# Where recurrent tiles, pairs of heads and w1's first factors stand in the second half of an input projection

## The chip, the cores and the metric

The kernel runs on one core of a Trainium2 chip. The metric is the device time of one execution in microseconds. The core has five engines with a queue each: TensorE (PE; its weight loads are shown as PEld), VectorE (DVE), ScalarE (ACT), GpSimd (POOL) and SyncE (SP, which here only starts DMA transfers). Each engine works through its own instructions in the order of the program, and a wait of one instruction holds up all that stand behind it on that engine.

## The reference, cut to what matters

One decoder block on 2048 tokens of width 1024, in float32. Eight attention heads and a gated linear recurrence share an input projection and an output projection; a squared-ReLU MLP follows.

```python
def hybrid_mixer(h, w_in, conv_w, conv_b, w_r, b_r, w_i, b_i, lam, w_out):
    z = h @ w_in
    q, k, v, xr, gr = jnp.split(z, [512, 1024, 1536, 2048], axis=-1)
    attn = dilated_attention(q, k, v)
    xr = causal_depthwise_conv(xr, conv_w, conv_b)
    rec = rg_lru(xr, w_r, b_r, w_i, b_i, lam) * jax.nn.gelu(gr)
    return jnp.concatenate([attn, rec], axis=-1) @ w_out

h = rms_norm(x, mix_norm_pre);  m = hybrid_mixer(h, ...);  x = x + rms_norm(m, mix_norm_post)
h = rms_norm(x, mlp_norm_pre);  x = x + rms_norm(squared_relu_mlp(h, w1, w2), mlp_norm_post)
```

## The kernel before, in words

A float32 product is made of three products on TensorE: each operand is split into a high part (a rounded copy, made by ACT) and a low part (the difference, made by DVE or POOL), and hi·hi, hi·lo and lo·hi are added up. `product` (L190 to L201) makes one tile z of 128 columns of the projection by 512 tokens: 8 steps over the width times 3, so 24 matmuls.

The sequence is handled in two halves of 1024 tokens, two blocks of 512 each. The steps of the input projection are named by strings. `q` with a half and a pair of heads (`qkv`, L203) makes the pair's six tiles: q, k and v, two blocks each. Each z is evacuated to zn by DVE (L225, L228), q and k are split into zh (ACT) and zl, and both are stored to DRAM by SP (L235, L236); v is transposed on PE (L240), split and stored. zh and zl have one buffer each. `r` with a half and a tile (`recurrent`, L288) does one of four recurrent tiles of 128 channels: per block a product for xr, its convolution (POOL L307, DVE L310 three times), two small matmuls for the gates (pr L313, pi L315), activations on ACT, a scan on DVE (L331), and a second product for the gate gr (L335), whose GELU runs mostly on POOL (L338 to L340) and whose result POOL stores. `a` with a pair is attention of the first half. For each step the raw columns of the weights (wraw, 256 KB at a time) are loaded by SP and split into wH (ACT) and wL. The engine of the low splits of weights and of zl is `pj.lo`: POOL at first, DVE once it is set so.

The program of this part is put in order by a scheduler, engine by engine, from the order in which the steps are written. The steps stand in three strings, `ORDER` (up to `a3`), `BETWEEN` and `LATER`. Behind `ORDER` the attention's memory is closed, and a pool `g2` opened in its place: the tiles of `early_factors` live there.

Two more things belong to this stretch. `load_wo(0)` loads w_out's first copy, eight transfers of 512 KB on SP (L781), and splits them (ACT woH, DVE woL); its memory is that which `lst.close()` frees. The output projection, whose first product is m0_0_0 (L846), needs it. `early_factors(j)` for j = 0 and 1 makes sums and differences of quarters of w1 for the MLP that comes later: four loads er of 256 KB (SP, L993), four sums (DVE, L1008 and L1013), seven splits into high and low (ACT and DVE), and fourteen stores sf (POOL, L1004) of 256 KB. `copies` are 40 transfers from DRAM to DRAM that lay out w_out and w2, issued by POOL (L1536) a few behind each step.

Behind this stretch the columns of the mix are loaded (m0_..L, SP L818), and the rest of the block (output projection, MLP, attention of the second half) follows by an order written out by hand.

Of the kernel before, what the change touches and what calls it, by code (L numbers as in the profile page):

```python
# [37 lines left out]
def f32(ap):  # L38
    return ap.bitcast(F32)
# [12 lines left out]
def split(nc, hi, lo, src, lo_eng=None):  # L52

    return (nc.scalar.copy(out=hi, in_=src),  # L54
            (lo_eng or nc.vector).tensor_tensor(out=lo, in0=src, in1=f32(hi), op=ALU.subtract))  # L55
# [708 lines left out]
def split_there(nc, hi, lo, lo_eng=None):  # L764

    split(nc, hi, lo, f32(lo), lo_eng)
# [44 lines left out]
def mix_columns(nc, sh, scr, hf, order, t):  # L811

    mx = {}
    for g0 in range(0, KT, 4):
        n = f"{hf}_{t}_{g0}"
        hi, lo = sh.pair(f"m{n}", (P, 4, P))
        k0 = order[g0]
        sh.mixed = nc.sync.dma_start(out=f32(lo), in_=scr["mix"][hf][k0:k0 + 4, :, t * P:(t + 1) * P].rearrange("k p t -> p k t"))  # L818
        split_there(nc, hi, lo, nc.vector if hf and t == 0 else nc.gpsimd)
        for i, k in enumerate(order[g0:g0 + 4]):  # L820
            mx[k] = (hi[:, i, :], lo[:, i, :])
    return mx
# [164 lines left out]
def early_factors(nc, sh, scr, w1, j):  # L987

    v, g = nc.vector, nc.gpsimd
    raw = [sh.s(f"er{j}_{i}", (P, KH, P)) for i in range(4)]  # L990
    a11, a12, a21, a22 = raw
    for i, t in enumerate(raw):
        nc.sync.dma_start(out=t, in_=w1[2 * j + i // 2][:, (i % 2) * KH:(i % 2 + 1) * KH])  # L993
    yield
    f = {}

    def made(m, src=None):
        if src is None:
            split_there(nc, *f[m])
        else:  # L1000
            f[m] = sh.pair(f"e{j}_{m}", (P, KH, P))
            split(nc, *f[m], src)
        for d, t in zip(scr["f"][j, m], f[m]):
            g.dma_start(out=d, in_=f32(t).rearrange("p k t -> p (k t)"))  # L1004

    def sub(m, x, y, op=ALU.subtract):
        f[m] = sh.pair(f"e{j}_{m}", (P, KH, P))
        v.tensor_tensor(out=f32(f[m][1]), in0=x, in1=y, op=op)  # L1008

    sub(5, a21, a22, ALU.add)  # L1010
    sub(7, a11, a21)
    sub(6, f32(f[5][1]), a11)
    v.tensor_tensor(out=a21, in0=a12, in1=f32(f[6][1]), op=ALU.subtract)  # L1013
    made(7)
    yield
    made(6)
    made(5)
    yield
    for m, t in ((1, a11), (2, a12), (4, a22), (3, a21)):
        made(m, t)  # L1020
        yield
# [405 lines left out]
NJ = FT // 2  # L1427
# [5 lines left out]
def trunk(tc, x, xT, g1, g2, g3, g4, w_in, conv_w, conv_b, w_r, b_r, w_i, b_i, lam, w_out, w1, w2,  # L1433
          ident_d, sel_d, mask_a, mask_b, out):
    nc = tc.nc
    out = out[0].rearrange("(b m c) d -> b c m d", m=P, c=NC)

    def sb(name, side):
        return tc.tile_pool(name=name, bufs=1, side=side, reuse_waits="tile")
# [5 lines left out]
    with (  # L1445
# [16 lines left out]
        def halves(shape, dt, n, nm):  # L1462
            return [[d.tile(shape, dt, name=f"s{nm}{hf}_{i}") for i in range(n)] for hf in range(2)]

        scr = {
            "q": halves([2, 2, HD, HT], F32R, NP, "q"),
            "k": halves([2, 2, HD, HT], F32R, NP, "k"),
            "v": halves([HT, 2 * P], F32R, NP, "v"),
            "co": halves([2, 2, HT], F32, NP, "co"),
            "mix": [d.tile([KT, P, HT], F32, name=f"smix{hf}") for hf in range(2)],  # L1470
            "x2": [d.tile([P, D], F32, name=f"sx2{i}") for i in range(S // P)],
            "a": [[d.tile([P, 7, TB], F32, name=f"sa{hf}_{j}") for j in range(NJ)] for hf in range(2)],
            "b": [d.tile([P, 4, TB], F32, name=f"sb{j}") for j in range(NJ)],
# [10 lines left out]
        def bank(tag, name):  # L1484
            if tag in RINGS:
                turn[tag] += 1
                tag = RINGS[tag][turn[tag] % 3 - 1]
            return banks.tile([P, TB], F32, tag=tag, bufs=BANKS[tag], name=name)
# [3 lines left out]
        def load_wo(hf, between=lambda: None):  # L1492
            return load_w_out(tc, wst.enter_context(sb(f"wo{hf}", "right")), scr["wout"], hf, order, cst, between)

        with contextlib.ExitStack() as st:
            p1a = st.enter_context(sb("p1a", "left"))
            p1 = st.enter_context(sb("p1", "left"))
            lst = contextlib.ExitStack()
            pl = lst.enter_context(sb("lru", "left"))
            pj = Project(tc, p1, p1a, pl, bank, cst, scr, x, xT, g1, w_in)  # L1500
            pj.recurrent_consts(conv_w, conv_b, w_r, b_r, w_i, b_i, lam)
            with sb("x0", "right") as px:
                w = {12: pj.load_start(12, px)}
                w[16] = pj.load_w(0, 16, nc.vector, px)
                w[13] = pj.load_w(0, 13, nc.vector, px)
                pj.load_norm(0, px)
                w[17] = pj.load_w(0, 17, nc.gpsimd, px)
                pj.spread_norm(0)
                pj.load_x(1, px)
                pj.load_norm(1, px)  # L1510
                pj.spread_norm(1)
                pj.recurrent(0, (0, 1), w, px)
                pj.load_norm(2, px)
                pj.load_norm(3, px)
            products = [(t[0], *map(int, t[1:])) for t in f"{ORDER} {BETWEEN} {LATER}".split() if t[0] in "qr"]

            copies = [(scr["wout"][k], w_out[k]) for k in order]
            for j in range(NJ):
                copies += [(scr["w2"][j][:, 0], w2[2 * j][:, 0:TB]),
                           (scr["w2"][j][:, 1:3], w2[2 * j + 1].rearrange("p (a d) -> p a d", a=2))]  # L1520

            def run(steps):
                for kind, *arg in [(t[0], *map(int, t[1:])) for t in steps.split()]:
                    if kind == "q":
                        pj.qkv(*arg)
                    elif kind == "r":
                        pj.recurrent(arg[0], (arg[1],))
                    elif kind == "a":
                        attend(*arg)
                    else:  # L1530
                        pj.load_x(*arg)
                        pj.spread_norm(*arg)
                    n = 8 if kind == "r" and arg[0] else 1 if len(copies) > 2 * NJ else 0
                    with tc.issue_after(cst["pool"].ins):
                        for dst, src in copies[:n]:
                            nc.gpsimd.dma_start(out=dst, in_=src)  # L1536
                    del copies[:n]
                    if kind in "qr":
                        products.pop(0)
                        if products:  # L1540
                            nxt, hf, i = products[0]
                            pj.load_ahead(hf, i if nxt == "q" else 12 + i)

            place = {"S": ("B", "B"), "pT": ("T", "T"), "o": ("O", "T")}
            with sb("at0", "right") as pa:
                attend = attention(tc, pa, lambda k, n: bank(place[k][0], n), cst, scr, 0, mask_a, mask_b, pa)
                run(ORDER)
            pg = per.enter_context(sb("g2", "right"))
            sh = Shared(pg, bank)
            run(BETWEEN)  # L1550
            lst.close()
            wo = load_wo(0)
            pj.lo = nc.vector
            early = [early_factors(nc, sh, scr, w1, j) for j in range(2)]
            for step in LATER.split():
                run(step)
                for _ in range(5):
                    if early and next(early[0], True):
                        early.pop(0)
            for rest in early:  # L1560
                for _ in rest:
                    pass
            ready = [mix_columns(nc, sh, scr, 0, order, t) for t in range(2)]
        sh.px = per.enter_context(sb("px", "left"))

# [49 lines left out]
        with per, tc.manual_schedule(engines={mybir.EngineType.PE}):  # L1615
            end = half(0, wo, ready)
            with sb("y0", "left") as pl, sb("z0", "left") as p:
                rest = mlp_out(tc, sh, p, cst, scr, 0, w2, g4, out, pl)
# [22 lines left out]
            with sb("y1", "left") as pl, sb("z1", "left") as p:  # L1641
                rest = mlp_out(tc, sh, p, cst, scr, 1, w2, g4, out, pl)
# [7 lines left out]
FIRST = 0  # L1650
SH = 2
ORDER = "q00 r02 q01 a0 r03 q02 a1 q03 x2 x3 a2 q10 a3"
BETWEEN = "r10 r11 r12 r13"
LATER = "q11 q12 q13"


def _by_residue(t):
# [51 lines left out]
```

## Time and profile before

| | us |
|---|---|
| median of three runs | 2258.18 |
| the runs | 2260.91, 2258.18, 2255.2 |
| the profiled execution, its own time | 2260.29 |
| its span | 2258.5 |
| first product of r10, of q11, of the output projection | 365.6, 520.2, 635.8 |

The mean granted clock of TensorE is 0.984. The page gives the busy time of each engine over the whole span; the stretch that the change touches is 366 to 636 us, some 12% of it, and is read by windows. There, r10 to r13 run up to 520 us, with attention's last pair beside them, and q11 to q13 behind. The program's names have the half, tile and block in them: z1_15_0 is the product of half 1, column tile 15 (12 to 15 are xr of r10 to r13, 16 to 19 their gates; 1, 5 and 9 are q, k and v of pair 1), block 0.

### The profile page before, as it was taken

What the parts mean: (1) busy time and instruction counts of PE and PEld (TensorE: products, weight loads), DVE (VectorE), ACT (ScalarE), POOL (GpSimd) and SP (SyncE); (2) the same over time, 40 slices, a digit from 0 to 9 for tenths busy, and PEclk for the clock granted to TensorE, in tenths of its full rate; (3) what the DMA queues carried; (4) which work ended last, traced back from release to release, by engine and by line L of the source; (5) the groups of instructions that cost most, each with busy time, mean ns of one, the idle gap of its engine ahead of it and who ended that gap; (6) DMA issues with size and microseconds to landing.
All of it is one profiled execution on the core that took longest, in us unless ns stands there. A gap on an engine that the chain in (4) does not pass through costs nothing.

```text
span 2258.5 us, 30786 instructions
## 1 busy us (share of the span) xinstructions
PE 2173.0 (96%) x10264; PEld 1778.9 (79%) x10264; DVE 1508.6 (67%) x2908; ACT 1232.9 (55%) x2489; POOL 449.6 (20%) x541
## 2 busy tenths in 40 slices
PE   8999999989899999998999999889999999999998
PEld 6678878767788788887878887778878888888887
DVE  6757475987648777774667676776766556646456
ACT  7647464654434555554766665754455555654442
POOL 5543415454223001011001111103200000000003
PEclk9999999999999999999999999999999999999999
DMA  8365674645974677869677787867553444776665
GB/s 289 95 189 179 183 233 151 188 143 184 330 227 171 232 264 274 309 257 303 193 208 215 215 242 195 230 211 235 175 192 137 168 140 163 262 238 194 196 192 182
DMA packets 223313, 473.51 MB, mean 210 GB/s; under 512 B 23105, under 2 KB 77793, under 8 KB 216881
## 3 DMA queue, kind: packets, MB, share of 16 engines
q1 hardware_dynamic: 194384, 336.87, 47.8%
q0 software_dynamic: 28768, 134.66, 17.1%
q8 instruction: 81, 1.33, 0.2%
q14 instruction: 80, 0.65, 0.1%
HBM read 337.09 MB, written 151.13 MB: 216 GB/s over the span
## 4 chain that ended last, share of the span: by engine, by line
PE 72%; DVE 8%; DMA 7%; issue 4%; ACT 4%; SPq 1%; POOL 0%; DVEq 0%; ACTq 0%; POOLq 0%
PE o L1210 8%; PE o L1211 8%; PE o L1212 7%; PE za L1061 5%; PE za L1062 5%; PE za L1060 5%; PE z L198 3%; PE z L199 3%; PE z L200 3%; PE m L846 3%; PE m L848 3%; PE m L847 3%; PE zc L1061 2%; PE zc L1062 2%; PE zc L1060 2%
## 5 line engine op out<-in xcount | busy, mean ns | idle before, releaser
L198 PE MATMUL z<-hH,wH 128*128 128x512 f32 x640 | 261.9, 409 | 17.5 <-ACT wH L54 7.0
L199 PE MATMUL z<-hL,wH 128*128 128x512 f32 x640 | 260.0, 406 | 0.6 <-DVE hL L173 0.6
L200 PE MATMUL z<-hH,wL 128*128 128x512 f32 x640 | 258.8, 405 | 0.5 <-DVE wL L55 0.5
L198 PEld LDWEIGHTS z<-hH,wH 128*128 128x128 f32 x640 | 122.4, 191 | 53.6 <-ACT wH L54 7.4
L200 PEld LDWEIGHTS z<-hH,wL 128*128 128x128 f32 x640 | 122.3, 191 | 30.3 <-issue 4.5
L199 PEld LDWEIGHTS z<-hL,wH 128*128 128x128 f32 x640 | 122.4, 191 | 30.2 <-issue 3.9
L420 ACT ACTIVATE smB<-smB,stB 128x128 f32<-128x128 f32 (+3 forms) x128 | 71.6, 560 | 82.0 <-DVE stB L414 81.8
L1065 ACT ACTIVATE sq<-sq 128x512 f32<-128x512 f32 x93 | 58.8, 632 | 89.6 <-DVE sq L1069 89.6
L55 POOL TENSOR_TENSOR wL<-wraw,wH 128x512 fp32r<-128x512 f32 x58 | 82.3, 1435 | 77.0 <-ACT wH L54 50.0
L55 DVE TENSOR_TENSOR tlB<-pT_B,thB 128x384 fp32r<-128x384 f32 x96 | 57.1, 598 | 53.0 <-ACT thB L54 48.9
L1125 POOL DMA_DIRECT2D sa<-sq x31 | 16.5, 532 | 363.1 <-ACT sq L1066 352.5
L54 ACT CAST wH<-wraw 128x512 fp32r<-128x512 f32 (+1 forms) x81 | 47.2, 611 | 61.6 <-DMA wraw<-in_dram 30.8
L420 ACT ACTIVATE sm<-sm,stA 128x256 f32<-128x256 f32 (+1 forms) x128 | 63.1, 495 | 29.4 <-DVE stA L414 29.2
L1066 ACT ACTIVATE sq<-sq 128x512 f32<-128x512 f32 x124 | 76.2, 629 | 1.9
L1244 POOL TENSOR_TENSOR y<-y,g4b 128x512 f32<-128x512 f32 x8 | 12.4, 1579 | 259.4 <-ACT junk_y L84 259.4
L414 DVE CUSTOM_DVE_ANT_0 smB<-SB,mask_b 128x128 f32<-128x128 f32 (+3 forms) x128 | 59.3, 483 | 6.3 <-PE pT_B L393 5.3
L629 PE MATMUL oB<-thB,vb 128*128 128x256 f32 x192 | 48.6, 282 | 11.3 <-ACT thB L54 10.4
L54 ACT CAST thB<-pT_B 128x384 fp32r<-128x384 f32 x96 | 48.5, 510 | 18.4 <-PE pT_B L393 10.1
L55 DVE TENSOR_TENSOR tlA<-pT,thA 128x512 fp32r<-128x512 f32 (+1 forms) x64 | 42.3, 669 | 22.0 <-ACT thA L54 21.7
L393 PE MATMUL pT_B<-ident,smB 128*128 128x128 f32 x320 | 52.2, 279 | 2.6 <-DVE tlB L55 1.8
L414 DVE CUSTOM_DVE_ANT_0 sm<-S,mask_a 128x256 f32<-128x256 f32 (+1 forms) x128 | 47.4, 409 | 9.1 <-PE pT L393 4.0
L1061 PE MATMUL za<-hLT,f_5H 128*128 128x512 f32 x128 | 50.1, 391 | 2.0 <-DVE hLT L55 2.0
(606 smaller groups left out, 7054.6 us busy)
## 6 DMA issues: line engine op xcount, KB each, us to landing
sa<-as POOLq DMA_DIRECT2D x31, 1024.0 KB, 6.1
w1r<-in_dram SPq DMA_DIRECT2D x56, 512.0 KB, 3.7
sa<-sq POOLq DMA_DIRECT2D x31, 768.0 KB, 4.0
wraw<-in_dram SPq DMA_DIRECT2D x79, 256.0 KB, 3.5
place<-in_dram SPq DMA_DIRECT2D x14, 1024.0 KB, 7.2
sb<-place POOLq DMA_DIRECT2D x14, 1024.0 KB, 5.3
kh<-sk SPq DMA_DIRECT2D x24, 512.0 KB, 5.0
kl<-sk SPq DMA_DIRECT2D x24, 512.0 KB, 6.8
```

The costliest lines, as they stand in the source:

```text
L55: (lo_eng or nc.vector).tensor_tensor(out=lo, in0=src, in1=f32(hi), op=ALU.subtract))
L198: pe.matmul(z, hi[:, k, :], hh, start=(k == 0), stop=False)
L199: pe.matmul(z, hi[:, k, :], hl, start=False, stop=False)
L200: pe.matmul(z, lo[:, k, :], hh, start=False, stop=(k == KT - 1))
L414: v.tensor_tensor_reduce(out=sm[:, c0:c0 + w], in0=sp[:, c0:c0 + w], in1=mask[:, mask.shape[-1] - w:], scale=1.0, scalar=3.0e38, op0=ALU.a ...
L420: s.activation(out=sm[:, c0:c0 + w], in_=sm[:, c0:c0 + w], func=AF.Exp, scale=-1.0, bias=st[:, 0, u, cols[j]:cols[j] + 1], accum_out=st[:, ...
L1060: pe.matmul(o, hi[:, k], bh[:, k], start=start and k == 0, stop=False, skip_group_check=True)
L1061: pe.matmul(o, hi[:, k], bl[:, k], start=False, stop=False, skip_group_check=True)
L1062: pe.matmul(o, lo[:, k], bh[:, k], start=False, stop=k == KH - 1, skip_group_check=True)
L1210: pe.matmul(o, ah[:, ts], bh, start=fresh and j == 0, stop=False, skip_group_check=True)
L1211: pe.matmul(o, ah[:, ts], bl, start=False, stop=False, skip_group_check=True)
L1212: pe.matmul(o, al[:, ts], bh, start=False, stop=j == NJ - 1, skip_group_check=True)
```

## The change

The steps behind attention stood as r10 r11 r12 r13 | q11 q12 q13, with `load_wo`, the change of `pj.lo` to DVE and the early factors at the bar; the factors' pieces were written one after each step behind the bar and the rest at the end. Now they stand as r10 q11 r11 q12 r12 r13 | q13; the factors for j = 0 are written whole behind q11, those for j = 1 behind q12, and at the bar stay `load_wo`, `lst.close()` and the change of `pj.lo`. So q11's and q12's low splits of weights and zl are POOL's. The copies are issued six behind each step from q10 on, before eight behind each r of half 1.

```diff
-                    n = 8 if kind == "r" and arg[0] else 1 if len(copies) > 2 * NJ else 0
+                    n = 1 if len(copies) > 2 * NJ else 6 if kind in "qr" and arg[0] else 0
...
-            run(BETWEEN)
+            early = [early_factors(nc, sh, scr, w1, j) for j in range(2)]
+            for step in BETWEEN.split():
+                run(step)
+                for _ in early.pop(0) if step in ("q11", "q12") else ():
+                    pass
             lst.close()
             wo = load_wo(0)
             pj.lo = nc.vector
-            early = [early_factors(nc, sh, scr, w1, j) for j in range(2)]
-            for step in LATER.split():
-                run(step)
-                for _ in range(5):
-                    if early and next(early[0], True):
-                        early.pop(0)
-            for rest in early:
-                for _ in rest:
-                    pass
+            run(LATER)
...
-BETWEEN = "r10 r11 r12 r13"
-LATER = "q11 q12 q13"
+BETWEEN = "r10 q11 r11 q12 r12 r13"
+LATER = "q13"
```

On SP, before, w_out's loads (woL0_k) stand between q11's last stores and w1's first quarters (er0):

```order
L235 DMA sk1_1_84<-zh1_5_1_5557 64x512
L236 DMA sk1_1_84<-zl1_5_1_5558 64x512
L110 DMA wraw1_6_0_5771<-in_6_dram 128x512
L110 DMA wraw1_6_1_5775<-in_6_dram 128x512
L781 DMA woL0_4_5374<-swo4_205 128x1024
L781 DMA woL0_5_5372<-swo5_206 128x1024
```

On SP, with the change, the same loads stand at the end, behind q13's stores and the mix's columns:

```order
L818 DMA m0_2_0L_6374<-smix0_103 128x4x128
L235 DMA sk1_3_86<-zh1_7_0_6114 64x512 x2
L818 DMA m0_2_4L_6379<-smix0_103 128x4x128
L236 DMA sk1_3_86<-zl1_7_0_6115 64x512 x2
L235 DMA sk1_3_86<-zh1_7_1_6149 64x512 x2
L236 DMA sk1_3_86<-zl1_7_1_6150 64x512 x2
L781 DMA woL0_4_5966<-swo4_205 128x1024
L781 DMA woL0_5_5964<-swo5_206 128x1024
```

w_out has moved behind the stores of k of pair 3 (sk1_3), and behind m0_2_4L, which waits until the last store of a factor (sf of j = 1) has landed.

On SP, with the change, w1's quarters come behind the gate's weights of r13 (19) and the first of q13 (3):

```order
L110 DMA wraw1_19_0_5753<-in_6_dram 128x512
L110 DMA wraw1_19_1_5757<-in_6_dram 128x512
L110 DMA wraw1_3_0_5939<-in_6_dram 128x512
L993 DMA er0_0_4995<-in_15_dram 128x512
L993 DMA er0_1_4996<-in_15_dram 128x512
```

Before, they stood behind the w_out loads, ahead of q12's last weights; their tiles lie in the memory that attention's last pair used.

On DVE, before, the end of the factors of j = 0 lies among q12's work:

```order
L55 TENSOR_TENSOR e0_4L_5942<-er0_3_5660,e0_4H_5941 128x512
L55 TENSOR_TENSOR wL1_3_5932<-wraw1_3_0_5933,wH1_3_5931 128x512
L55 TENSOR_TENSOR wL1_3_5932<-wraw1_3_1_5937,wH1_3_5931 128x512
L228 TENSOR_TENSOR zn1_10_0_5884<-z1_10_0_5859,bc2_3290 128x512
L55 TENSOR_TENSOR e0_3L_5948<-er0_2_5659,e0_3H_5947 128x512
L55 TENSOR_TENSOR zl1_6_0_5807<-zn1_6_0_5804,zh1_6_0_5806 128x512
```

On DVE, with the change, the end of the factors of j = 1 lies among r13's work, ahead of the first zn of q13:

```order
L331 SCALAR_TENSOR_TENSOR xc1_3_0_5790<-r1_3_0_5799,state_278,i1_3_0_5801 128x512
L55 TENSOR_TENSOR wL1_7_6078<-wraw1_7_0_6079,wH1_7_6077 128x512
L55 TENSOR_TENSOR e1_4L_5542<-er1_3_5502,e1_4H_5541 128x512
L310 SCALAR_TENSOR_TENSOR xc1_3_1_5878<-xr1_3_1_5874,cw_222,xc1_3_1_5878 128x512
L55 TENSOR_TENSOR wL1_7_6078<-wraw1_7_1_6083,wH1_7_6077 128x512
L225 SCALAR_TENSOR_TENSOR zn1_3_0_6032<-z1_3_0_6007,bc2_3290 128x512
L332 COPY state_278<-xc1_3_0_5790 128x1
L310 SCALAR_TENSOR_TENSOR xc1_3_1_5878<-xr1_3_1_5874,cw_222,xc1_3_1_5878 128x512
```

Both blocks of factors now stand between the first convolution of r13 and that zn. On PE the order is the same up to r10's first product, and as long up to m0_0_0 but for one transpose; z1_3_0, z1_3_1, z1_7_0 and z1_7_1 of q13 follow each other in one and the same bank, since the other bank of products holds z1_19_1 until its evacuation (gr1_3_1), which stands late on DVE.

## The prediction

> **What bounds the kernel now.** I read the page's first part, then the windows by stage, then the waits of TensorE (PE), then single instructions.
>
> ```profile
> PE 2173.0 (96%) x10264; PEld 1778.9 (79%) x10264; DVE 1508.6 (67%) x2908; ACT 1232.9 (55%) x2489; POOL 449.6 (20%) x541
> ```
>
> PE is busy 96% of the 2258.5 us span, so a gain can only come from its gaps. The change reorders what runs between the first product of r10 (365.6 us) and the first product of the output projection (635.8). The windows cut that stretch at the starts of r10, r11, r12, r13, q11, q12 and q13 (columns: window, its length, then busy time of PE, PE's weight loads, VectorE = DVE, ScalarE = ACT, GpSimd = POOL, granted PE clock, DMA share, GB/s):
>
> ```profile
> 366.00:400.00 34.00, 34.00 (x182) 28.36 (x181) 23.98 (x49) 19.30 (x42) 16.85 (x20) 1.00 0.41 128
> 400.00:440.00 40.00, 37.56 (x211) 30.10 (x210) 35.15 (x81) 26.71 (x63) 12.56 (x12) 1.00 0.55 151
> 440.00:475.00 35.00, 30.79 (x134) 22.30 (x133) 31.98 (x48) 18.76 (x36) 27.29 (x30) 1.00 0.58 189
> 475.00:520.00 45.00, 37.36 (x189) 29.27 (x188) 39.21 (x69) 28.10 (x55) 23.51 (x28) 0.92 0.40 122
> 520.00:558.00 38.00, 38.00 (x182) 30.25 (x181) 28.10 (x46) 16.65 (x27) 15.09 (x15) 1.00 0.65 203
> 558.00:594.00 36.00, 33.79 (x147) 26.74 (x147) 26.69 (x43) 18.45 (x33) 10.35 (x17) 1.00 0.93 320
> 594.00:636.00 42.00, 38.08 (x159) 30.55 (x158) 16.86 (x27) 11.33 (x20) 10.37 (x17) 0.92 0.93 303
> sum 270.00, PE 249.58 PEld 197.57 DVE 201.97 ACT 139.31 POOL 116.01; mean PE 35.65 PEld 28.22 DVE 28.85 ACT 19.90 POOL 16.57
> ```
>
> Lost to PE: 270.0 − 249.6 = 20.4 us idle, and the clock at 0.92 in two windows, 0.08 × (45 + 42) = 7.0 us: **27.4 us** in all. Of these 17.9 lie in r11 to r13 (2.4 + 4.2 + 7.6 + 3.6) and 9.5 in q12 and q13 (2.2 + 3.9 + 3.4). In r11 to r13 DVE is busy 35.15 of 40, 31.98 of 35, 39.21 of 45. The waits of PE from 360 to 640 (line <- releaser: total, times, longest):
>
> ```profile
> PE pr L313 <- DVE xc L310: 5.8, 1, 5.8
> PE z L198 <- DVE zn L228: 3.9, 1, 3.9
> PE z L198 <- DVE gr L335: 1.9, 2, 1.5
> PE z L198 <- DVE xr L304: 1.7, 4, 0.9
> PE z L198 <- ACT wH L54: 1.7, 1, 1.7
> ```
>
> PE waits for DVE: in the r steps because DVE is saturated there, in q13 (3.9) for another reason, which the DVE's own rows show:
>
> ```profile
> 591.38 0.68 DVE L55 TENSOR_TENSOR e_3L<-er,e_3H 128x512 fp32r<-128x512 f32 x1
> 602.68 0.69 DVE L55 TENSOR_TENSOR zl<-zn,zh 128x512 fp32r<-128x512 f32 x1 [10.62 <-DMA sq<-zl]
> 603.48 0.69 DVE L228 TENSOR_TENSOR zn<-z,bc 128x512 f32<-128x512 f32 x1
> ```
>
> DVE sat 10.6 us in its queue on a zl split, whose single buffer was still being stored; the zn behind it held PE's bank.
>
> **The change part by part.** *Alternation.* q11 and q12 each need less of DVE than of PE (28.1 of 38, 26.7 of 36 above, the latter with w_out's and w1's splits in it). With one between each two r steps, DVE catches up. What stays in r10 to q12 I work out from one recurrent block (DVE's groups from 440 to 540 us, POOL's from 366 to 520: line, operation, tiles, count | busy, mean ns | idle before):
>
> ```profile
> L310 DVE SCALAR_TENSOR_TENSOR xc<-xr,cw,xc 128x512 f32<-128x512 f32 x15 | 14.2, 947 | 0.1
> L331 DVE TENSOR_TENSOR_SCAN xc<-r,state,i 128x512 f32<-128x512 f32 x6 | 8.7, 1447 | 0.1
> L329 DVE SCALAR_TENSOR_TENSOR i<-i,xc 128x512 f32<-128x512 f32 x5 | 6.3, 1261 | 6.5 <-ACT i L320 6.5
> L343 DVE SCALAR_TENSOR_TENSOR ge<-ge,xc 128x512 f32<-128x512 f32 x5 | 6.2, 1234 | 0.0
> L327 DVE SCALAR_TENSOR_TENSOR th<-a,th 128x512 f32<-128x512 f32 x5 | 4.9, 971 | 0.1
> L326 DVE TENSOR_TENSOR a<-r 128x512 f32<-128x512 f32 x5 | 4.7, 931 | 0.7 <-ACT r L324 0.7
> L304 DVE TENSOR_TENSOR xr<-z,bc 128x512 f32<-128x512 f32 x4 | 4.3, 1077 | 0.0
> L330 DVE TENSOR_TENSOR i<-i,th 128x512 f32<-128x512 f32 x5 | 3.8, 766 | 0.0
> L55 POOL TENSOR_TENSOR wL<-wraw,wH 128x512 fp32r<-128x512 f32 x16 | 22.9, 1450 | 13.7 <-ACT wH L54 13.6
> L307 POOL TENSOR_SCALAR xc<-xr,cw,vec_cb 128x512 f32<-128x512 f32 x8 | 7.9, 988 | 6.0 <-DVE xr L304 5.9
> ```
>
> From a product's end to pr: 1.08 + 0.99 + 3 × 0.95 = 4.9 us. One product takes 5.6 us when nothing disturbs it (first and last of its 24 matmuls; the last two rows of this fence are the clock's after a gap and in q13's undisturbed end):
>
> ```profile
> 629.84 0.40 PE L198 MATMUL z<-hH,wH 128*128 128x512 f32 x1
> 635.21 0.39 PE L200 MATMUL z<-hH,wL 128*128 128x512 f32 x1
> 600.00:610.00 10.00, 6.08 (x18) 4.61 (x17) 7.13 (x12) 3.79 (x7) 1.59 (x3) 0.66 0.89 280
> 620.00:630.00 10.00, 10.00 (x44) 8.08 (x43) 1.20 (x3) 0.62 (x1) 0.00 (x0) 1.00 0.89 296
> ```
>
> So the chain hides behind the product that stands between, if DVE is on time. I leave about 1 us for each of the four blocks of r11 and r12, and 1 for a weight split like the 1.7 above: **5 us**. Below it is bounded by 2 (r10's window has no idle time at all), above by 9, half of what r11 to r13 lost.
>
> *zl and w splits to POOL.* q11's and q12's 8 zl and 12 wL splits leave DVE for POOL (20 × 1.45 = 29 us, in some 75 us). They hide behind products; and a zl that waits for its store no longer stands in DVE's queue. Without that cover each costs at most its 1.45 us once per weight, within the 9. The copies go out six a step from q10 on, before eight a step from r10 on, and stay hidden in POOL's idle time.
>
> The Trainium skill has a rule against this part: by its page "GPSIMD Engine Reference" (sections "1. Specifications" and "8. Key points"), GpSimd shares its SBUF interfaces with VectorE and contends with DVE instructions that have two SBUF inputs. The trace agrees as far as it goes: L310 takes 947 ns here, in windows where POOL computes, while the same size takes 0.68 us in e_3L's row above. By this rule DVE would be slowed 1.4 times under 29 us of POOL work, by some 8 us; without it by nothing.
>
> DVE has that time: 9.9 and 9.3 us idle in the two windows. The 9.5 us of q12 and q13, though, come back in other places, since w_out and w1's factors now meet r13 and q13.
>
> *w1's factors in r13.* The order on SP puts er0's loads behind the raw weights of r13 and q13, so they land some 8 us into r13. Let T be the start of r13's first product. The two blocks of factor work on DVE, eleven operations each, stand behind xc of 1_3_0 and around the scan of 1_3_0. One operation starts 0.60 us after the last (first two of the block in before):
>
> ```profile
> 580.96 0.69 DVE L1008 TENSOR_TENSOR e_5L<-er,er 128x512 f32<-128x512 f32 x1 [1.22 <-DMA er<-in_dram]
> 581.57 0.68 DVE L1008 TENSOR_TENSOR e_7L<-er,er 128x512 f32<-128x512 f32 x1
> ```
>
> Step by step: r13's first xc is done at T + 5.6 + 4.9 = 10.5. e0: 11 × 0.6 = 6.6, between them th, a, ge and i of 1_2_1 (0.97 + 0.93 + 0.7 + 1.26 = 3.9) and about 1.4 of waiting for ACT: 22.4. Then gr, xr, i, scan, ge (0.7 + 1.08 + 0.77 + 1.45 + 1.23 = 5.2): 27.6. Ten of e1's eleven operations (6.0), a, th, i, i, scan of 1_3_0 (0.93 + 0.97 + 1.26 + 0.77 + 1.45 = 5.4), two L310 (1.9), two wL and zn of q13 (2.0): zn1_3_0 ends at about T + 43. PE meanwhile has five products (28.0), four pr or pi (pi's eight records below are four blocks', 4.1 / 4 = 1.0, some of it beside other work; I take 0.9: 3.6), a wait of 2.4 for xc (which stands behind ACT's work for 1_2_1) and of 1.3 for gr: its z1_3_0 ends at T + 35.3.
>
> ```profile
> L315 PE MATMUL pi<-xc,bd_i 128*128 128x512 f32 x8 | 4.1, 598 | 0.0
> ```
>
> The next product must have the same bank, so it **waits 7.9 us**, where before it waited 3.9. After the 3.9 us gap the clock fell to 0.66 in the window of 600, 3.4 us; I take 2.9 here. Three more handings-on of that bank (before z1_7_0, z1_7_1 and z1_11_0) cost an operation of 0.68 each: 2.0. Sum: 2.4 + 1.3 + 7.9 + 2.9 + 2.0 = **16.5 us**.
>
> *w_out.* Before, its eight loads were issued behind q11's stores, their last split ended 57 us ahead of need:
>
> ```profile
> 559.51 10.16 SPq L781 DMA_DIRECT2D woL<-swo  x8
> 574.49 3.85 DVE L55 TENSOR_TENSOR woL<-woL,woH 128x512 fp32r<-128x512 f32 x6 [0.66 <-ACT woH L54]
> 570.00:580.00 10.00, 10.00 (x45) 8.08 (x44) 8.97 (x15) 6.05 (x11) 0.00 (x0) 1.00 0.98 351
> ```
>
> From 559.5 to 578.3 they took 18.8 us, at a DMA share of 0.98. Now they stand on SP behind the zl stores of 1_7_1, and behind m0_2_4L's load, which waits for the last factor store. 1_7_1's product ends at about T + 65; with zn, the zl split behind the one before it, and its store, the first w_out load is issued near T + 71. By 18.8 us the last split ends at T + 90; at 4 MB over 351 GB/s (11.9) and 3 for the splits, at T + 86. PE has 62.3 us of work from T on (ten products, 56.0; six pr or pi, 5.4; the transposes of v, 0.9) and comes to the output projection at T + 78.8 and needs the eighth factor 4.9 us later, at 83.7. Wait: 2.3 to 6.5, I take **4.5 us**.
>
> *Sum.* 27.4 removed; 5 + 16.5 + 4.5 = 26 put in their place: **1.4 us gained**, of the profiled execution's 2260.29 (span 2258.5). The median, 2258.18, is 2.1 lower; I subtract from it: 2256.8, say 2257. Bounds: at 0.68 an operation the recurrent ones are 4 us shorter up to zn1_3_0; with no loss of clock (2.9) and the short w_out wait, the tail is 21 − 4 − 2.9 − 2.2 = 12, and with 2 for the first part the gain is 13. At the other end the 21 factor operations run at 947 instead of 600 ns (7 us) and w_out waits 6.5: 30, with 9 in the first part 39, a loss of 12.
>
> **Rivals.** *The tail is short* (gain 13, **2245 us**): DVE has slack ahead of r13, so it starts there with nothing left over, and POOL mostly issues DMAs then, at which the e rows stay at 0.68. Against it: the fixed order and the single bank.
>
> *w_out decides* (slower, **2270 us**). Place: SP's queue ahead of the eight loads. From a first issue at T + 71 on, each us late is a us of PE's, and 6.8 us slower than before needs T + 79. What is late is the last factor store, on which m0_2_4L's load waits. Before it went out at 616.82 and took about 8 us, that is 55 us from er0's first load to its landing:
>
> ```profile
> 570.20 4.01 SPq L993 DMA_DIRECT2D er<-in_dram  x4
> 616.82 0.54 POOL L1004 DMA_DIRECT2D sf<-e_3L  x1 [0.42 <-DVE wL L55]
> sf<-e_3L POOLq DMA_DIRECT2D x2, 256.0 KB, 8.2
> ```
>
> With er0 at T + 2.4 this would be T + 57. It decides from T + 64, since the zl stores behind it take some 7 us more. If it lands at T + 77, 13 late, the time is 2256.8 + 13 = 2270. For it: the stores share the DMA with the wider traffic of q13; against it: 7 us of slack.
>
> *The alternation relieves nothing*: attention's third pair still runs beside r10 to r12, and POOL's 29 us slow DVE there. If r10 to q12 keep the 17.9 us of r11 to r13, time is 2256.8 + 12.9 = 2270. Against: PE's waits above name DVE, and q steps leave it idle. The rule of "GPSIMD Engine Reference" named above is this rival's, and the 0.95 against 0.68 us is all that the trace has for it.
>
> *It does not do what it says*: the factors are written behind q11 and q12, but stand behind r13's first xc on DVE. The time of that is already in the sum.
>
> **How the numbers follow.** Forecast 0.42; short tail 0.33; w_out 0.17; no relief 0.08. A measurement of this kernel tells about 0.3% from no change, 6.8 us. Faster by more: 0.34, all but a little of it the short tail; within: 0.41; slower: 0.25, the last two rivals. The range goes from 2241 to 2271: the bounds of the sum, a little further on the faster side for what the first part may give beyond 2; the forecast alone is 2250 to 2264.
>
> **What would show it.** Windows over r11 and r12 with PE over 95% busy: the alternation works; under 90%: no relief. The waits of PE in r13 and q13: z L198 <- DVE zn L225 of about 8 us once, pr <- xc of about 2.4. Under 3 us there, the tail is short. The first m L846 behind ACT or DVE wo L54/L55, or the DMA woL: 2 to 7 us as forecast, over 12 the slower rival. e operations starting 0.6 us apart: my price; 0.9: the upper bound. Above all wrong I would be if DVE came to r13 late, since every term there begins with its xr.

## The result and the profile after

The changed kernel takes 2270.47 us (median of 6, 2267.58 to 2281.33) where the kernel before takes 2256.69 (median of 6, the three runs shown above among them): a ratio of **1.0056, 95% interval 1.0038 to 1.0074**. It is slower by about 12.6 us by this ratio, 13.8 by the medians. The forecast was 2257, no change, in a range that reached to 2271: the time lies at the range's far end, and the forecast itself did not come.

The profiled execution has a span of 2265.8 us. The table of its windows is cut at the starts of r10, q11, r11, q12, r12, r13 and q13 (columns as before: window, length, busy time of PE, weight loads, DVE, ACT, POOL, granted clock, DMA share, GB/s):

```profile
363.00:390.00 27.00, 27.00 (x127) 21.69 (x125) 12.34 (x19) 9.45 (x13) 14.07 (x19) 1.00 0.54 187
390.00:448.00 58.00, 55.36 (x317) 46.15 (x316) 44.23 (x113) 37.25 (x98) 24.98 (x23) 0.97 0.66 200
448.00:478.00 30.00, 28.81 (x144) 23.21 (x143) 13.27 (x26) 12.01 (x26) 18.58 (x17) 1.00 0.44 141
478.00:527.00 49.00, 47.35 (x254) 38.11 (x253) 32.56 (x66) 26.66 (x59) 25.09 (x28) 1.00 0.63 191
527.00:551.00 24.00, 24.00 (x104) 18.97 (x104) 15.79 (x21) 7.18 (x12) 16.70 (x14) 1.00 0.44 138
551.00:589.00 38.00, 29.27 (x103) 20.81 (x102) 33.21 (x43) 18.46 (x27) 24.99 (x31) 0.87 0.69 235
589.00:642.00 53.00, 42.45 (x159) 31.91 (x158) 31.66 (x43) 22.59 (x35) 21.61 (x26) 0.90 0.74 230
```

Two things are to be seen. In the first five rows, r10 to r12, PE is idle for 5.5 us of 188 and its clock costs 1.7 more (0.03 × 58): the alternation keeps PE busy, 7.2 us lost. In the last two, r13 and q13, 8.7 + 10.6 us are idle and the clock costs 0.13 × 38 + 0.10 × 53 = 10.2: **29.5 us lost** in 91. The waits of PE from 360 to 700 us say on what:

```profile
PE z L198 <- DVE gr L335: 7.0, 3, 3.1
PE z L198 <- DVE state L332: 5.6, 1, 5.6
PE pr L313 <- ACT i L320: 4.8, 1, 4.8
PE m L847 <- DVE woL L55: 1.6, 7, 0.2
PE vt L240 <- DVE vs L55: 1.5, 1, 1.5
```

The wait of the gate's product (gr) comes three times, and the 5.6 us put down to `state` are a wait for zn1_3_0, which ends beside it (rows further below). The first output product is stretched by its waits for w_out's splits: it takes 9.3 us (642.16 to 651.43) where the next one takes 5.5, 3.8 more. So the loss is 7.2 + 29.5 + 3.8 = 40.5 us in place of 27.4, 13.1 more, about the change of the median. (Such sums count idle time inside a slow stretch of the clock twice: by the rows about 1.7 us here and 1.6 in the 27.4, so the difference stands. The two profiled executions differ by 7.3 us only: from r10's first product to the second output product this one takes 11.9 us longer, but it was 2.3 us ahead at r10's start already, and some 2 us came back behind.)

### The profile page after: what moved, and what is told of

Its sections match the earlier page's. It is cut to its first block, busy times and chain, and to the rows that moved or that the text cites. A ratio compares the mean times of both kernels' runs of the same rounds, so it can differ in the third digit from the quotient of the medians.

```text
span 2265.8 us, 30778 instructions
## 1 busy us (share of the span) xinstructions
PE 2173.3 (96%) x10264; PEld 1777.0 (78%) x10264; DVE 1492.4 (66%) x2888; ACT 1231.5 (54%) x2489; POOL 477.1 (21%) x561
## 4 chain that ended last, share of the span: by engine, by line
PE 60%; DVE 7%; DMA 6%; issue 4%; ACT 4%; POOL 1%; SPq 0%; DVEq 0%; ACTq 0%; POOLq 0%
PE o L1210 7%; PE o L1211 7%; PE o L1212 7%; PE za L1061 5%; PE za L1062 5%; PE za L1060 5%; PE zc L1061 2%; PE zc L1062 2%; PE zc L1060 2%; PE m L848 2%; PE m L847 2%; PE m L846 2%; PE oB L629 1%; PE z L198 1%; PE z L200 1%
## 5 line engine op out<-in xcount | busy, mean ns | idle before, releaser
L55 POOL TENSOR_TENSOR wL<-wraw,wH 128x512 fp32r<-128x512 f32 x70 | 99.7, 1441 | 89.9 <-ACT wH L54 61.2
L1125 POOL DMA_DIRECT2D sa<-sq x31 | 16.5, 533 | 362.4 <-ACT sq L1066 351.9
L414 DVE CUSTOM_DVE_ANT_0 smB<-SB,mask_b 128x128 f32<-128x128 f32 (+3 forms) x128 | 59.4, 483 | 10.6 <-PE pT_B L393 9.1
L629 PE MATMUL oB<-thB,vb 128*128 128x256 f32 x192 | 49.5, 287 | 12.9 <-ACT thB L54 11.9
L629 PEld LDWEIGHTS oB<-thB,vb 128*128 128x128 f32 x192 | 38.2, 199 | 18.8 <-ACT thB L54 14.9
```

What stands on the lines that cost most here:

```text
L629: pe.matmul(dst.rearrange("p (i m) -> p i m", m=P), vb[:, x * NC + c, :], t[:, cols].rearrange("p (i m) -> p i m", m=P)[:, ::step], start= ...
```

## The experiments

Three theories were put to the chip. **F**: w1's factors, set among r13's operations on DVE and ACT, hold PE. **W**: w_out's late loads hold it. **G**: GpSimd's tensor work slows DVE. All ratios are against the kernel before, run beside each experiment.

### Without the factors, their stores kept (e1, e2)

```diff
-    raw = [sh.s(f"er{j}_{i}", (P, KH, P)) for i in range(4)]
...
+    e = sh.s(f"er{j}_0", (P, KH, P))
+    nc.vector.memset(e, 0.0)
+    yield
+    for m in (7, 6, 5, 1, 2, 4, 3):
+        for d in scr["f"][j, m]:
+            nc.gpsimd.dma_start(out=d, in_=e.rearrange("p k t -> p (k t)"))
```

> The changed order, but w1's first factors are not made: no quarter of w1 is loaded, DVE does none of their 22 operations and ACT none of their 14 casts; the 28 stores stay and write a constant, so the MLP's result is not the reference's. Theory F (the factors' work on DVE and ACT stands between r13's own operations, and holds PE's pr, gr and zn): the waits and slow clock between r13's first product and the output projection fall from about 33 us to 8 to 12, the time from 2270 to 2245 to 2250. Rival W (w_out's late loads hold the end): 3 us at most, 2265 or more. Rival G (GpSimd's own tensor work slows DVE in r13): r13 keeps its waits, 2262 or more.

> The order before, with the same left out. Theory F: the factors stood under cover there, so the time falls by 0 to 4 us, to 2253 to 2257 (the wait of 3.9 us in q13 came from the store of zl). If the factors cost as much in both orders, it falls by as much as e1 does, some 20 us, and theory F is wrong in its place.

Measured: e1 1.0061 (1.0037 to 1.0085), e2 1.0045 (1.0022 to 1.0068). Theory F's numbers failed in both. The time of e1 lies where W and G had put it, but not for their reasons: the profile shows that the experiment brought a new cause. The waits of PE in e1 from 540 to 760 us, and a stretch of SP's queue:

```profile
PE pr L313 <- DVE xc L310: 26.8, 2, 24.0
...
591.20 20.70 SPq L110 DMA_DIRECT2D wraw<-in_dram  x4
```

Nothing paces the 28 stores any longer: POOL issues them in one train, from 564.6 to 585.7 us, ahead of r13's L307 in its own queue, and the next raw weights take 20.7 us to be issued. The runs say nothing on F. They show that the factors' arithmetic also spreads 7 MB of stores (28 of 256 KB) over time.

### Without the factors, their places filled early (e5, e6)

```diff
+            given = [(d, w1[m][:, 0:KH].rearrange("p k t -> p (k t)")) for j in range(2)
+                     for m in (7, 6, 5, 1, 2, 4, 3) for d in scr["f"][j, m]]
-                        for dst, src in copies[:n]:
+                        for dst, src in copies[:n] + given[:3]:
-            early = [early_factors(nc, sh, scr, w1, j) for j in range(2)]
...
```

> The changed order, w1's factors not made at all in this stretch: their 28 places in DRAM are filled early, three copies from w1 behind each of the steps up to a3, so the MLP's result is not the reference's. Theory F (the factors' work on DVE and ACT in r13 holds PE): the tail's waits and slow clock fall from 33 us to 8 to 12, the time is 8 to 13 us below the kernel before. Rival C (r13's own chain of xr, xc, gates and scan with one bank of products is enough to hold PE): 20 us or more stay, the time is that of the kernel before or up to 10 us above it.

> The order before, with the factors left out in the same way (early copies, no work). Theory F: they were under cover there, 0 to 5 us below the kernel before. If it falls by as much as e5 against the changed kernel, the place of the factors is not what cost.

Measured: e5 1.0044 (1.0027 to 1.0061), e6 1.0056 (1.0033 to 1.0079). Against both expectations the times went up, because the early copies cost in the steps up to a3: r10's first product starts at 377.1 us in e5 and at 381.0 in e6, where it started at 363.3 and 365.7. The stretch under study can still be read by itself, from r10's first product to the first of the output projection, in one profiled execution each:

| | with the factors | without | factors cost |
|---|---|---|---|
| order before | 365.65 to 635.79: 270.1 | 380.96 to 646.43 (e6): 265.5 | 4.6 |
| changed order | 363.33 to 642.16: 278.8, and 3.8 in the next product | 377.11 to 639.75 (e5): 262.6, and 0.8 in the next product | 19 |

Two readings. The factors cost 4.6 us under the cover they had, and 19 where the change puts them: some 14 us more, and the change cost 12.6. So F is right in size. And without the factors the changed order is only 2 us shorter than the order before, though the sum had 27.4 us of loss removed against 5 left in r10 to r12. Both are differences of single executions; two executions of one and the same kernel further below (e9 and e13) differ by 1.4 us in this stretch. The windows of e5 over r13 and q13, with its waits from 360 to 760, show what is left:

```profile
563.00:600.00 37.00, 28.24 (x104) 20.96 (x105) 26.20 (x29) 16.65 (x24) 19.87 (x20) 0.86 0.21 68
600.00:640.00 40.00, 38.07 (x156) 29.30 (x155) 28.73 (x40) 21.11 (x32) 8.06 (x8) 0.96 0.51 160
...
PE pr L313 <- DVE xc L310: 8.8, 1, 8.8
```

Counted as above the two steps lose 17.5 us, neither the 8 to 12 of F nor the 20 or more of rival C. Half of it is one wait of 8.8 us in r13. On DVE (first fence) and POOL (second) there stands:

```profile
563.26 7.71 DVE L310 SCALAR_TENSOR_TENSOR xc<-xr,cw,xc 128x512 f32<-128x512 f32 x2 [0.71 <-POOL xc L307]
```

```profile
564.29 1.28 POOL L55 TENSOR_TENSOR m_4L<-m_4L,m_4H 128x512 fp32r<-128x512 f32 x1
565.52 2.48 POOL L55 TENSOR_TENSOR wL<-wraw,wH 128x512 fp32r<-128x512 f32 x2
567.96 1.25 POOL L55 TENSOR_TENSOR m_0L<-m_0L,m_0H 128x512 fp32r<-128x512 f32 x1
569.17 1.25 POOL L55 TENSOR_TENSOR m_4L<-m_4L,m_4H 128x512 fp32r<-128x512 f32 x1
```

Two operations of 0.7 us take 7.7, until shortly after POOL's train of five ends at 570.4. Three of the five are splits of the mix's columns (m), which POOL does in the changed kernel only from 613.8 us on: without the factors their loads come at 551 us instead of 607. So this wait is in part a product of the experiment, and it is not shown that r13 would lose as much in the changed kernel. It opened theory G anew, in another form.

### The low parts on DVE (e3)

```diff
+            pj.lo = nc.vector
             early = [early_factors(nc, sh, scr, w1, j) for j in range(2)]
             for step in BETWEEN.split():
```

> The changed kernel with the low splits of weights and zl on DVE from r10 on instead of from q13 on, so that GpSimd does no splits in that stretch. Theory F: the factor work in r13 stays, and DVE gets more work in r10 to r13: 2268 to 2282. Rival G: DVE is no longer slowed by GpSimd, 2255 to 2262.

Measured: 1.0086 (1.0066 to 1.0106), 2280.77 us: in F's range. Giving the splits of weights and zl to DVE makes it slower; GpSimd keeps the gate's work and the splits of the mix's columns. From 360 to 660 us PE waits 15.7 us at one place:

```profile
PE z L198 <- DVE gr L335: 21.2, 2, 15.7
```

DVE isn't full there: in r13 (555 to 593 us of e3) it is busy 25.5 of 38 us. What holds gr is the order of its queue: a weight split, now DVE's, waits until 564.9 for its raw weights, and nine operations of the factors stand between it and gr at 575.9. So the run shows another cost of giving DVE the splits. It doesn't settle G.

### Fewer pairs between, two behind (e4), and r10 earlier (e8)

```diff
-BETWEEN = "r10 r11 r12 r13"
-LATER = "q11 q12 q13"
+BETWEEN = "r10 q11 r11 r12 r13"
+LATER = "q12 q13"
```

> The order r10 q11 r11 r12 r13, then w_out, w1's factors and q12 q13, written as before (copies and engine of the low parts too). Theory F: r11 to r13 keep about two thirds of their loss (12 of 17.9), the factors lie behind r13 with two pairs as cover: 2248 to 2257. Rival W: w_out's loads stand late on SP, behind q13's first store, and hold the output projection by 5 to 10 us: 2260 to 2266.

Measured: 1.0064 (1.0046 to 1.0081), 2275.24 us: a miss for F's number and for W's. Its waits from 540 to 760 us:

```profile
PE pr L313 <- DVE state L332: 8.2, 1, 8.2
PE z L198 <- ACT e_6H L54: 3.0, 1, 3.0
PE z L198 <- DVE zn L228: 2.3, 1, 2.3
PE m L846 <- ACT m_0H L54: 2.2, 1, 2.2
```

The three r steps in a row lose no less than before: pr waits 8.2 us here and 6.2 once more ahead of this window (to 522.7), where its longest wait in the kernel before was 5.8. The two pairs behind them, with the factors and w_out beside them, lose in three more places.

```diff
-ORDER = "q00 r02 q01 a0 r03 q02 a1 q03 x2 x3 a2 q10 a3"
-BETWEEN = "r10 r11 r12 r13"
+ORDER = "q00 r02 q01 a0 r03 q02 a1 q03 x2 x3 a2 r10 q10 a3"
+BETWEEN = "r11 r12 r13"
```

> The kernel before with r10 ahead of q10 and a3, beside attention's third pair instead of behind it. If DVE's saturation in r10 to r13 is what costs, one r step less there gives back 3 to 8 us. If attention beside r10 loses as much, no change or up to 5 us slower.

Measured: 1.0070 (1.0044 to 1.0096), 14 us slower, worse than either side gave. Of its waits from 360 to 660 us the largest are 7.2 (vt behind a split of v), 4.2 (pr behind the scan's state), 3.7 (zn) and 3.5 (pi behind ACT), spread over the stretch. No single cause was isolated.

### Factors held back behind r13 (e11, e12)

```diff
     for i, t in enumerate(raw):
+        v.tensor_copy(out=t[:, 0, 0:1], in_=gate[:, 0:1])
         nc.sync.dma_start(out=t, in_=w1[2 * j + i // 2][:, (i % 2) * KH:(i % 2 + 1) * KH])
...
```

> The changed order, but w1's factors are held back by their data: each tile of a quarter first gets one column copied from the last gate gr of r13, so that their loads, DVE's 22 operations and ACT's 14 casts stand behind r13 and among q13's work; w_out's loads come behind them, the mix's columns behind w_out. Theory F: r13 runs as in the experiment without factors, and q13's DVE has room: 6 to 15 us below the changed kernel, so within 5 us of the kernel before. If w_out and the factors' DMA hold the output projection then: m L846 or L847 waits over 8 us, and the time is that of the changed kernel.

> Both: factors held behind r13, gate on ACT and DVE. F and G2 together: 3 to 8 us below e11, 2 to 8 us below the kernel before.

Measured: e11 1.0131 (1.0100 to 1.0163), 2290.13 us, and e12 1.0129 (1.0091 to 1.0166), 2290.42. In e11 r13 runs better, as F had it, but the time is 20 us above the changed kernel: the wait of L847 that the expectation named came, and is longer. e12 is no faster than e11, so its expectation failed. Windows of e11 over r13, q13, and the stretch behind (626 to 664), the wait behind them, and SP's w_out loads:

```profile
555.00:582.00 27.00, 25.42 (x103) 18.88 (x102) 21.75 (x26) 12.45 (x17) 15.50 (x15) 1.00 0.35 108
582.00:626.00 44.00, 39.47 (x154) 30.13 (x152) 32.87 (x53) 20.24 (x30) 17.14 (x24) 0.92 0.59 197
626.00:664.00 38.00, 3.07 (x8) 1.89 (x9) 19.56 (x31) 16.04 (x29) 9.58 (x16) 0.56 0.98 343
...
PE m L847 <- ACT m_0H L54: 26.4, 1, 26.4
...
629.75 6.57 SPq L782 DMA_DIRECT2D woL<-swo  x8
```

Up to the end of q13's last product at 625.5, r13 and q13 now lose 1.6 + 4.5 us and 0.08 × 44 of clock, 9.6 instead of 29.5: most of that loss came with the factors' place in r13. But then PE stands still for some 35 us, while the DMA is at 0.98. Of these, 8.9 are a wait of q13's last transposes, whose v split stands on DVE among the second block of factors; 26.4 are the wait for the mix's columns. The second block's stores and w_out are moved there (w_out's last split begins at 653.1), and the mix's columns stand on SP behind them and behind the last store of v, so that their load is issued at 656.4 only: that end of the wait is the experiment's own order. In the kernel before, w_out and the factors began at 559.5 and had 76 us at a share of 0.93 until the output projection. So the reason that seems to lie below F is cover. The factors are 2 MB of loads and 7 MB of stores, and w_out, whose memory r13 has to free, is 4 MB; by the stretch before they fit under some 70 us of other work (an estimate), and the changed order has one pair behind r13, 42 us before, to give. That no place in the changed order would serve is not shown: two were tried. Put in r13, the factors hold PE by DVE and ACT; put behind it, they hold it by the DMA and the queues.

### zl on GpSimd (e7)

```diff
-                    self.cst["pool"] = split(nc, zh, zl, zn, lo_eng=self.lo)[1]
+                    self.cst["pool"] = split(nc, zh, zl, zn, lo_eng=nc.gpsimd)[1]
```

> The kernel before with one thing changed: the low part zl of q11 to q13 is made by GpSimd, not DVE, so a zl that waits for its buffer's store stands in GpSimd's queue. If the 3.9 us wait of q13 and the slow clock behind it (3.4) come from DVE's queue, 4 to 8 us below the kernel before. Rival: the wait goes to another place (GpSimd's factor stores, DVE beside a busy GpSimd): no change, within 3 us.

Measured: 1.0033 (1.0019 to 1.0048), 6 us slower, where one side gave 4 to 8 below and the other no change. The rival's mechanism is what is seen: PE's wait grew from 3.9 us to 6.7 (waits from 360 to 760; then POOL's queue, then DVE's):

```profile
PE z L198 <- DVE zn L228: 6.7, 1, 6.7
...
631.22 1.26 POOL L55 TENSOR_TENSOR m_0L<-m_0L,m_0H 128x512 fp32r<-128x512 f32 x1 [10.74 <-ACT m_0H L54]
...
633.73 0.69 DVE L228 TENSOR_TENSOR zn<-z,bc 128x512 f32<-128x512 f32 x1 [13.52 <-POOL zl L55]
```

In POOL's queue the zl of q13 stands behind a split of the mix's columns, which waits 10.7 us for its high part; DVE's next zn waits for that zl, and PE's bank for the zn. So the expected gain was eaten by another wait of the same kind. It is 2.8 us of the 6; of the rest, the same profile shows 2.5 at a transpose of v, and pr in r10 to r13, which this edit does not touch, waits 8.4 where it waited 5.8.

### The gate's work off GpSimd (e9, e13, e10, e14)

```diff
-        g.tensor_tensor(out=ge, in0=gr, in1=gr, op=ALU.mult)
-        g.tensor_scalar(out=ge, in0=ge, scalar1=0.044715, scalar2=1.0, op0=ALU.mult, op1=ALU.add)
-        g.tensor_tensor(out=ge, in0=ge, in1=gr, op=ALU.mult)
+        s.activation(out=ge, in_=gr, func=AF.Square, scale=0.044715 ** 0.5)
+        v.scalar_tensor_tensor(out=ge, in0=ge, scalar=1.0, in1=gr, op0=ALU.add, op1=ALU.mult)
```

> The kernel before, with GpSimd's three operations on the gate (square, scale and add, product: L338 to L340, about 2.9 us a block) replaced by a Square on ACT and one operation on DVE; the result is the same in another rounding. Theory G2 (a DVE operation that meets GpSimd's tensor work waits until that work ends; in the profile before, operations that overlap it are stretched by 31.9 us in all between r10 and the output projection, those that don't by 0.6): with some 23 us of GpSimd's work out of r10 to r13 the stretch falls to 20 or less, and the time by 3 to 8 us below the kernel before. Rival: DVE's count of operations is what fills r10 to r13: no change, or slower, by the 0.6 us a block that DVE gets in addition.

> The kernel of e9 again, with more rounds, beside e14. G2 (GpSimd's tensor work stretches DVE's operations in r10 to r13): 2 to 8 us below the kernel before, with an interval clear of 1. If e9's difference was chance: within 2 us.

> The changed kernel with the same gate on ACT and DVE. G2: 3 to 8 us below the changed kernel, 3 to 9 us above the kernel before. Theory F says the factors still stand in r13 and q13: not below the kernel before.

> The kernel of e9 with the first term of the convolution (L307, 0.8 us a block on GpSimd) on ACT too, so that GpSimd is left with the weights' and zl's low parts. G2: DVE's stretch falls again, by some 3 us; the time is 0 to 4 us below e13. Rival: ACT's queue (weight casts, tanh, table loads) makes xc later, and pr waits for it: 0 to 6 us above e13.

On the kernel before: e9 0.9979 (0.9959 to 0.9999), e13, the same again with more runs, **0.9981 (0.9964 to 0.9997)**, 2253.53 beside 2258.87 us. Both lie where G2 had put them, e13 with an interval just clear of 1. The stretch of DVE's operations between r10 and the output projection (each one's time above the median of its form in the same trace, a slightly smaller measure than that of the 31.9) fell from 28.8 to 16.7 us in e9 and 19.4 in e13, though DVE got one operation a block more. From r10's first product to the output projection the profiled executions take 266.0 us (e9) and 267.5 (e13), where the kernel before took 270.1. This fits theory G, by a small amount. It doesn't prove it: the edit also shortens the gate's chain and frees POOL's queue, and it acts on the recurrent tiles of the first half too. It is the only version here that beats both kernels. On the changed kernel (e10) it did nothing that can be measured: 1.0051 (1.0034 to 1.0068) against 1.0056; the expected 3 to 8 us did not come, and F's side of the expectation did. e14 is 1.0149 (1.0129 to 1.0170), but not by the stretch under study: that is no longer there than in e13 (271 us from the last product ahead of r10 to the output projection, against 273). It loses at the program's start, where ACT's casts of weights come late (waits from 0 to 120 us):

```profile
PE z L198 <- ACT wH L54: 25.6, 4, 16.0
```

So it does not answer whether L307 on ACT helps in r10 to r13.

Two parts of the change were not tried alone: the new pacing of the copies, and the splits of q11 and q12 on POOL while the factors stand in r13.

## Why the prediction was wrong

**What bounds, and the alternation.** That PE waits for DVE in r10 to r13 held. r10 to r12 lost 7.2 us where I had put 5, within its bounds of 2 and 9. But I counted all of the 27.4 us as gone with the order, and put only the factors' terms in r13 and q13. Without factors e5 gains only 2 us net on e6, and r13 and q13 still lose 17.5 us in e5 and, up to 625.5 us, 9.6 in e11. Both experiments brought waits of their own, so how much r13 loses by itself stays open.

**The step that failed** is the tail, w1's factors in r13: I had 16.5 us, the windows show 29.5. (In the working, 43 − 35.3 is 7.7, not 7.9; that changes nothing.) Term by term, with these rows of the changed kernel (PE, then DVE, then ACT):

```profile
576.77 2.08 PE L313 MATMUL pr<-xc,bd_r 128*128 128x512 f32 x2 [4.77 <-ACT i L320]
581.23 0.80 PE L198 MATMUL z<-hH,wH 128*128 128x512 f32 x1 [2.39 <-DVE gr L335]
601.61 0.79 PE L198 MATMUL z<-hH,wH 128*128 128x512 f32 x1 [5.56 <-DVE state L332]
626.95 0.50 PE L198 MATMUL z<-hH,wH 128*128 128x512 f32 x1 [3.07 <-DVE gr L335]
```

```profile
571.83 0.68 DVE L327 SCALAR_TENSOR_TENSOR th<-a,th 128x512 f32<-128x512 f32 x1
...
577.36 3.22 DVE L55 TENSOR_TENSOR e_3L<-er,e_3H 128x512 fp32r<-128x512 f32 x1
580.50 0.68 DVE L335 TENSOR_TENSOR gr<-z,bc 128x512 f32<-128x512 f32 x1
...
600.87 0.68 DVE L225 SCALAR_TENSOR_TENSOR zn<-z,bc 128x512 f32<-128x512 f32 x1
```

```profile
567.94 0.62 ACT L54 CAST e_7H<-e_7L 128x512 fp32r<-128x512 f32 x1 [2.85 <-DVE e_7L L1008]
...
572.28 1.28 ACT L328 ACT_TABLE_LOAD   x1
...
574.73 1.28 ACT L320 ACT_TABLE_LOAD   x1
576.03 0.69 ACT L320 ACTIVATE i<-pi,vec_bi 128x512 f32<-128x512 f32 x1
```

- pr of 1_3_0 waited 4.8 us, not 2.4. ACT reached the i of 1_2_1 at 576.03, though PE had ended its pi at 568.7: the seven casts of e0, two table loads and two other operations stood ahead of it. I had priced ACT with 1.4 us. The casts are not all of it: one of the two others is th, which needs DVE's L327, and that ended at 572.5 only, behind five operations of the factors. By these rows the casts alone are about 1.6 us (an estimate).
- gr held a product three times, 7.0 us in all; I had 1.3, and 2.0 for the bank. Before the second, e_3L took 3.22 us instead of 0.68 beside two of POOL's weight splits (577.5 to 580.0). The other two are not the factors' directly: the first came at 558.8, ahead of their first operation, and the third at 627.0, behind DVE operations of 1.78 and 1.75 us beside POOL's splits of the mix's columns.
- zn1_3_0 held its bank's next product for 5.6 us; I had 7.9. It ended at 601.55, and the product began at 601.61. That mechanism was right and its size near.
- The clock cost 10.2 us (some 8.5 without the idle time in its slow stretches), and I had 2.9: one gap priced, four came. The windows:

```profile
581.00:587.00 6.00, 5.77 (x14) 4.57 (x15) 5.33 (x9) 2.31 (x3) 1.91 (x3) 0.50 0.97 342
601.00:607.00 6.00, 5.39 (x13) 4.23 (x14) 3.14 (x6) 0.62 (x1) 1.38 (x2) 0.50 1.04 388
627.00:632.00 5.00, 5.00 (x15) 3.96 (x16) 2.42 (x4) 0.62 (x1) 1.21 (x2) 0.66 0.45 119
```

- A split of v held a transpose for 1.5 us; not in the sum.

**w_out** cost 3.8 us where I had 4.5, but not for the reason that I gave, so that is luck in part. I had the 18.8 us of its transfers behind a first issue at T + 71. These rows show SP's loads, ACT's casts and DVE's splits:

```profile
631.81 12.49 SPq L781 DMA_DIRECT2D woL<-swo  x8
...
640.59 4.78 ACT L54 CAST woH<-woL 128x512 fp32r<-128x512 f32 x9
...
641.54 3.69 DVE L55 TENSOR_TENSOR woL<-woL,woH 128x512 fp32r<-128x512 f32 x6
```

The first load went out at 631.81, that is T + 80.5 with T = 551.3, later than I had it because the tail was longer. Six were issued within 3 us; the last two waited 8.4 us for the store of r13's last gate (smix<-ge) to land. And the casts began only behind the cast of the last v in ACT's queue (640.11), so that the output product met the splits one by one. The slower rival that I named, w_out behind the last factor store, is not what happened: that store was issued at 603.2. In e11, where the factors come later, the long wait is for the mix's columns.

**The rivals.** The price that I gave as the upper bound, 39 us of loss in place, is about what came (40.5), by luck. I had reached it with factor operations at 947 ns; most of them ran at their 0.60 us step, and the loss came instead from ACT's queue, the clock and the gates. "No relief" was wrong: in the window of r11 (448 to 478) PE is busy 96%, above the 95 that I had named as the sign.

## What to carry to other kernels

Before work is moved between stages, ask what it has been covering: behind r13 two pairs of heads covered some 13 MB of transfers, part of which could only start once r13 had freed its memory, and none of the orders tried here gave that cover back. A stall of PE has to be priced with the slow clock behind it, here some 2 to 4 us for each stretch that had gaps of 3.1 to 5.6 us. And a block of work set into a dependent chain costs on every engine that it touches: price its casts on ACT as well as its operations on DVE.

## What the runs showed of the hardware

A DVE operation that meets tensor work of GpSimd can be held until that work ends, at times for a whole train of it when the instructions follow each other. In the kernel before, a copy of 128x3 elements took 5.85 us (464.95 to 470.80), while POOL ran five operations on end:

```profile
464.95 5.85 DVE L305 COPY tail<-xr 128x3 f32<-128x3 f32 x1
```

```profile
464.47 1.29 POOL L710 TENSOR_TENSOR nb<-nb,co 128x512 f32<-128x512 f32 x1
465.71 1.29 POOL L340 TENSOR_TENSOR ge<-ge,gr 128x512 f32<-128x512 f32 x1
466.96 1.29 POOL L713 TENSOR_TENSOR na<-na,nb 128x512 f32<-128x512 f32 x1
468.22 2.54 POOL L55 TENSOR_TENSOR wL<-wraw,wH 128x512 fp32r<-128x512 f32 x2
```

Not every train holds so long: at 450.31 an L326 came in between two such POOL operations (450.31 to 451.74), and the second, a weight split, took 1.72 us where those above took about 1.28. Of the 24 L310 between r10 and the output projection, the 8 that overlap POOL's tensor work lose 5.7 us, the 16 others 0.1. The evacuations from the matmul's banks are not stretched (L335 0.67 to 0.71 us, L304 1.05 to 1.12). POOL's DMA issues cost nearly nothing in that trace (0.7 us over 68 DVE operations), but in e13 an L310 took 1.73 us and an L329 1.79 beside nothing else, so that stays open. The Trainium skill, in "Trainium Architecture — The Big Picture" (section "What this means for kernel authors"), has the port pair that DVE and GpSimd share under an exclusive lock, not a split of bandwidth. The traces agree with the lock; what happens over a train, only the traces here say. In the prediction I had taken the milder reading, a factor of 1.4.

After gaps of PE of 3.07 and 5.56 us its matmuls start about twice as far apart for some 3.4 and 5.8 us, at a granted clock of 0.50; after the two gaps of 4.77 and 2.39 us, close together, some 8 us of work are slow (windows above). The Trainium skill's "TensorE: Matmul & The Clock Gate" (Part 1) has half rate after an idle window of about 3.4 us, until about as long a time of work. Here a gap of 3.07 us sufficed, in e10 one of 2.49 (clock 0.57 from 559 to 563 us), and two of the slow stretches were over 5 us. A gap does not always do it: pr waits 3.41 us at about 97 us in both traces, and from 97 to 108 us the clock is 0.84 in the kernel before and 1.00 in the changed one.
